# Layer 0 of a two-layer diffusion step: two of four gate chunks computed beside later head groups, modulation pieces spread evenly, rotary products on VectorE

## The chip, the cores and the metric

The kernel runs on one core of one Trainium2 chip. The metric is device time in microseconds (us) from one launch. Engines are named as in the profile: PE is TensorE (PEld its weight load), DVE is VectorE, ACT is ScalarE, POOL is GpSimd, SP issues most transfers.

## The reference, cut to what matters

Tokens are 512 latent ones (four tiles of 128) and 128 context ones (a fifth tile), width 1024. Layer 0 is gated attention, layer 1 a linear recurrence. All of the change lies in layer 0.

```python
sh, sc, g = split(silu(cond) @ ada_w[i] + ada_b[i])        # per layer: 3 x 1024 values for each of two conditions
h = x * (1 + sc) + sh
q, k, v, gate = split(h @ w_in)                            # 1024, 256, 256, 1024 columns
q, k = rms_norm(q), rms_norm(k)                            # per head of 64; 16 query heads, 4 key heads
q, k = rope(q), rope(k)                                    # latent tokens only: x*cos + rotated(x)*sin
o = softmax(q @ k.T / 8) @ v                               # latent: 128 cached + 512 keys; context: 128 keys
x = layer_norm(alpha * x + g * ((o * silu(gate)) @ w_out))
```

## The kernel before, in words

Each float32 weight piece (128x1024, 512 KB) is loaded into a ring of three `raw` buffers and split into a rounded part `whi` (ACT, a cast) and a remainder `wlo` (a subtraction, `split_piece`, L217); each product is three matmuls. Projection weights come in chunks of 256 columns, two pieces each: chunk 0 to 3 are the queries of head groups 0 to 3 (four heads on one key head), chunks 6 to 9 the gate.

The program writes instructions in one order; a scheduler in the compiler may move them a little on each engine, and `keep_in_program_order` pins some. The stages of layer 0 are:

- **Start**: load, modulate, keys and values (`acc`), queries of group 0 (`pmm`, L323 to L325).
- **Lead-in** (`lead_in`): 16 blocks of gate projection (`gps`, L316 to L318, 24 matmuls of 320 columns each; four chunks, each two row halves by two token halves), each followed by a Silu on ACT (L705) into `gs`. Between the blocks the pieces of work in `later` are issued: for the queries of group 0 `rms_prep` (sum of squares on DVE, power -1/2 on POOL, L188, product `qn` on DVE, L518), `rope_apply` (`u` = x*sin on POOL, L531; `r` = x*cos and the sum on DVE, L533 and L535), `q_split`, then transposes (`qps`, `kps`) on PE.
- **Attention** (`att_gen`): for each of four groups one context unit and eight latent units. A unit has fronts (scores `sc`, maximum `nm` on DVE L802, exponential `p` on ACT L805, reciprocal `rc` on DVE, scaling of `p` on POOL L810), backs (transposes `pt` on PE L817, copied to `pts`), and for every second unit the product with the values (`pot`, L736) that is multiplied into `gs` on DVE (`av_out`, L740). Fronts run two units ahead.
- A second stream, `side`, is woven into attention by `weave`: after each step of attention an accumulator grows by `SIDE_B`, and each whole unit lets `side` take one step. It holds, in a row: query projection of group 1 (`q_gen`, `qmm`), four modulation chunks (`ada_gen`, `adaps`, two `raw` pieces each), group 2, four chunks, group 3, four chunks, four chunks, then the first two pieces of the output weights (`wohi`, `wolo`) and the splitting of `gs` into `hhi`, `hlo` (L923, L924).
- **Output projection** (`outp`, L969 to L971), and then layer 1.

PSUM in lead-in and attention: two double banks (`bank2`, scores), one bank for `pot`, three banks (`bank1`) for all else, `pt`, `qmm`, `adaps` and transposes among it.

Of the kernel before, what the change touches and what calls it, by code (L numbers as in the profile page):

```python
# [18 lines left out]
P = 128  # L19
# [14 lines left out]
ADA_CUT = (4, 8, 12)  # L34
# [7 lines left out]
D_LO = 1  # L42
ROOT = False
SIDE_T = 2.2
SIDE_B = 0.7
# [13 lines left out]
class Side:  # L59
# [5 lines left out]
    def step(self):  # L65
        while self.items:
            ready = self.items[0][2:]
            if ready and not ready[0]():
                return False
            try:  # L70
                next(self.items[0][1])
                return True
            except StopIteration:
                self.items.pop(0)
        return False

    def until(self, name):
        while any(i[0] == name for i in self.items):
            assert self.step()

    def finish(self):
        while self.step():
# [50 lines left out]
def hybrid_step(ctx: ExitStack, tc: tile.TileContext, a: dict, o: dict):  # L133
# [158 lines left out]
    def ada_gen(chunks):  # L292
        todo, last = None, None
        for l, c in chunks:
            ps = bank1("adaps")
            ada_mms(ps, l, c, 0)
            if last:
                last()
            last = todo and ada_out(*todo)
            yield  # L300
            ada_mms(ps, l, c, 1)
            yield
            todo = (l, c, ada_row(ps))
        if last:
            last()
        if todo:
            last = ada_out(*todo)
            yield
            if last:
                last()  # L310
                yield

    def feat_mms(ps, w, mt, j, hhi, hlo):
        c, t = slice(mt * P, (mt + 1) * P), slice(*HALVES[j])
        for k in range(KT):
            nc.tensor.matmul(ps[:, :320], w.hi(k)[:, c], hhi[:, k, t], start=(k == 0), stop=False)  # L316
            nc.tensor.matmul(ps[:, :320], w.hi(k)[:, c], hlo[:, k, t], start=False, stop=False)
            nc.tensor.matmul(ps[:, :320], w.lo(k)[:, c], hhi[:, k, t], start=False, stop=(k == KT - 1))  # L318

    def tok_gen(out, w, tt, hhi, hlo):  # L320
        t = slice(tt * P, (tt + 1) * P)
        for k in range(KT):
# [3 lines left out]
            if k % 4 == 3:  # L326
                yield
# [15 lines left out]
    ADA_AT = (0,) + ADA_CUT + (len(ADA),)  # L343
    ADA_B = [ADA[ADA_AT[n]:ADA_AT[n + 1]] for n in range(4)]

# [8 lines left out]
    for c in (0, 6, 7, 8, 9):  # L354
        order.extend(pieces("attn_w_in", c))
    for c in range(3):
        order.extend(pieces("attn_w_in", c + 1))
        order.extend(ada_pieces(ADA_B[c]))
    order.extend(ada_pieces(ADA_B[3]))
# [138 lines left out]
    def rms_prep(ps, n):  # L498
        return rms_apply(ps, n, rms_stat(ps, n, ROOT))

    def rms_stat(ps, n, root=False):
        w = n * CW
        sq = prep.tile([P, 2 * CW], F32, tag="sq", name="sq")
        nc.scalar.activation(sq[:, :w], ps[:, :w], AF.Square)
        ss = tiny.tile([P, 8], F32, tag="ss", name="ss")
        nc.vector.tensor_reduce(ss[:, :4 * n], view(sq, 0, [[HD, 4 * n], [1, HD]]), AX.X, ALU.add)
        rstd = tiny.tile([P, 8], F32, tag="rstd", name="rstd")
        if root:
            nc.scalar.activation(rstd[:, :4 * n], ss[:, :4 * n], AF.Sqrt, bias=eps[:, 0:1], scale=1.0 / HD)
            nc.vector.reciprocal(rstd[:, :4 * n], rstd[:, :4 * n])  # L510
        else:
            rsqrt(rstd[:, :4 * n], ss[:, :4 * n], 1.0 / HD, NORM_EPS)
        return rstd

    def rms_apply(ps, n, rstd):
        w = n * CW
        qn = prep.tile([P, 2 * CW], F32, tag="qn", name="qn")
        nc.vector.tensor_tensor(view(qn, 0, [[HD, 4 * n], [1, HD]]), ps[:, :w].rearrange("p (h d) -> p h d", d=HD),  # L518
                                view(rstd, 0, [[1, 4 * n], [0, HD]]), ALU.mult)
        return qn  # L520

    def rope_apply(qn, tt0, n, cos, sin, g, r=None):
# [8 lines left out]
        nc.gpsimd.tensor_tensor(heads4(u[:, :w], n), heads4(qn[:, :w], n),  # L531
# [55 lines left out]
    def q_gen(c, X):  # L587
        w = Weights("attn_w_in", c)
        yield
        yield  # L590
        pend = None
        for tt0, n in UNITS:
            ps = yield from tok_unit(w, tt0, n, "qmm")
            rstd = rms_stat(ps, n)
            yield
            if pend:
                for i in range(pend[1]):
                    pend[0](i)
                    yield
            qn = rms_apply(ps, n, rstd)  # L600
            r = rope_apply(qn, tt0, n, cosq, sinq, qg)
            yield
            pend = (q_split(r, tt0, n, c % 2, X, bank1), n)
        yield
        for i in range(pend[1]):
            pend[0](i)
            yield
# [11 lines left out]
    def lead_in(att):  # L619
# [40 lines left out]

        def q_job(n):
            tt0, m = UNITS[n]
            r = rope_apply(rms_prep(q0[n], m), tt0, m, cosq, sinq, qg)
# [21 lines left out]
        open_rest()  # L685
        k_rope(2)
        later = [lambda n=n: q_job(n) for n in range(3)] + [lambda: backs.append(split_k(ck, 1, 0))]
        later += [lambda n=n: k_split(n) for n in range(3)]
        step = 0
        for ch in range(6, 10):  # L690
            if ch < 9:
                ws[ch + 1] = Weights("attn_w_in", ch + 1, LEAD_LO)
            w = ws.pop(ch)
            for mt in range(2):
                for j, (t0, t1) in enumerate(HALVES):
                    ps = bank_any("gps")
                    feat_mms(ps, w, mt, j, hhi, hlo)
                    step += 1
                    if step % 2 or not later:
                        settle()  # L700
                    if step % 2 and later:
                        later.pop(0)()
                    if step > 16 - EARLY:
                        next(att)
                    nc.scalar.activation(gs[:, 2 * (ch - 6) + mt, t0:t1], ps[:, :320], AF.Silu)  # L705
# [32 lines left out]
    def av_out(pot, gt):  # L738
        tv = pot[:, :CW]
        nc.vector.tensor_tensor(gt, tv.rearrange("p (a b) -> p a b", a=2) if len(gt.shape) == 3 else tv, gt, ALU.mult)  # L740
# [11 lines left out]
    def prompt_unit(c):  # L752
# [29 lines left out]
        def apply():  # L782
            pot = pop[0].tile([P, 512], F32, tag="po", name="potp")
# [9 lines left out]
    def sample_unit(c, h, qh):  # L793
# [29 lines left out]
        def pair():  # L823
            mine = {k: live.pop(k) for k in list(live)}

            def apply():
                pot = pop[0].tile([P, 512], F32, tag="po", name="pot")
# [8 lines left out]
    def att_gen(side):  # L836
        units = []
        for c in range(4):
            units.append(prompt_unit(c))
            units += [sample_unit(c, 2 * pr + j, qh) for pr in range(2) for qh in range(2) for j in range(2)]  # L840
# [643 lines left out]
```

## Time and profile before

| | |
|---|---|
| time, median of 3 runs | 902.72 us (902.19 to 903.58) |
| the profiled execution, its own time | 903.73 us |
| its span, first to last instruction | 902.0 us |
| PE busy | 851.4 us (94%) |
| DVE, ACT, POOL busy | 533.7, 372.6, 245.9 us |
| mean granted clock of PE | 0.984 |

The span lies inside the execution's time; 1.7 us lie around it. A matmul's end is modelled in the profile, and matmuls overlap, so busy PE time says when it had work, not how fast it went; the pace is read from the distance of starts. The granted clock is a share of full speed: 1.00 is 2.4 GHz, 0.5 the lower level of 1.2 GHz.

### The profile page before, as it was taken

The page shows a single profiled execution, that of the slowest core. Times are in us where ns is not written, and L with a number is a line of the kernel's source. Part 1 is how long each engine was busy: PE and PEld are TensorE (multiplying, and loading weights), DVE is VectorE, ACT ScalarE, POOL GpSimd, SP SyncE. Part 2 cuts the span into 40 slices and gives each one's busy share as a digit, 9 for nine tenths or more (in the row PEclk, how much of TensorE's full clock was granted, in tenths as well). Part 3 has the DMA queues.
Part 4 walks back from the last instruction along what each step waited for, and adds up shares of the span by engine and source line. Part 5 has one row for each costly group of instructions (what it writes and reads, how often), then busy time and mean ns, then how long its engine had stood idle before and what let it go on. Part 6 is the DMA issues. An engine that isn't in the chain of part 4 may idle for free.

```text
span 902.0 us, 19259 instructions
## 1 busy us (share of the span) xinstructions
PE 851.4 (94%) x8116; PEld 745.8 (83%) x8116; DVE 533.7 (59%) x952; ACT 372.6 (41%) x735; POOL 245.9 (27%) x269
## 2 busy tenths in 40 slices
PE   5999899899899899999999999999999999998995
PEld 3679898778768766677889999999999999986774
DVE  3465334654554554577644667585858575859495
ACT  2141445454454655633244444444444444444200
POOL 2016012524434644440000133233232414120110
PEclk9999899999899999999999999999999999998998
DMA  9931220033033046173121322323132323223121
GB/s 319 324 112 37 92 70 25 2 115 121 1 114 121 1 162 212 48 238 135 57 94 48 96 84 78 100 78 94 54 115 65 90 88 88 84 71 136 54 94 70
DMA packets 32678, 89.86 MB, mean 100 GB/s; under 512 B 4400, under 2 KB 11568, under 8 KB 32592
## 3 DMA queue, kind: packets, MB, share of 16 engines
q1 hardware_dynamic: 21984, 71.57, 24.0%
q0 software_dynamic: 3264, 9.51, 3.9%
q10 hardware_dynamic: 7344, 7.55, 2.7%
q8 instruction: 64, 1.05, 0.5%
q14 instruction: 22, 0.18, 0.1%
HBM read 79.44 MB, written 9.18 MB: 98 GB/s over the span
## 4 chain that ended last, share of the span: by engine, by line
PE 76%; DVE 8%; POOL 6%; ACT 4%; DMA 3%; issue 2%; SPq 0%; ACTq 0%; DVEq 0%; POOLq 0%
PE rps L1091 7%; PE rps L1092 6%; PE rps L1093 6%; PE vgps L1081 5%; PE vgps L1082 4%; PE vgps L1083 4%; PE pot L736 3%; PE outp L969 3%; PE outp L970 3%; PE outp L971 3%; PE adaps L259 3%; PE pt L817 2%; PE lv L1221 2%; POOL rstd L188 2%; PE gps L316 2%
## 5 line engine op out<-in xcount | busy, mean ns | idle before, releaser
L1091 PE MATMUL rps<-h1hi,rhi 128*128 128x320 f32 x368 | 117.5, 319 | 0.0
L1092 PE MATMUL rps<-h1lo,rhi 128*128 128x320 f32 x368 | 113.7, 309 | 0.0
L1093 PE MATMUL rps<-h1hi,rlo 128*128 128x320 f32 x368 | 113.5, 308 | 0.0
L810 POOL TENSOR_SCALAR p<-p,rc 128x640 f32<-128x640 f32 x64 | 53.6, 840 | 84.2 <-DVE rc L809 83.0
L805 ACT ACTIVATE p<-sc,nm 128x640 f32<-128x640 f32 x64 | 51.0, 797 | 46.6 <-DVE nm L802 42.4
L1091 PEld LDWEIGHTS rps<-h1hi,rhi 128*128 128x128 f32 x368 | 69.1, 188 | 1.3
L1092 PEld LDWEIGHTS rps<-h1lo,rhi 128*128 128x128 f32 x368 | 69.1, 188 | 0.0
L1093 PEld LDWEIGHTS rps<-h1hi,rlo 128*128 128x128 f32 x368 | 69.1, 188 | 0.0
L1249 POOL COPY At<-near 32x160 f32<-32x160 f32 x32 | 14.0, 438 | 197.5 <-DVE near L1211 196.5
L217 DVE TENSOR_TENSOR rlo<-raw,rhi 128x1024 fp32r<-128x1024 f32 x32 | 46.1, 1441 | 34.0 <-ACT rhi L216 34.0
L802 DVE TENSOR_REDUCE nm<-sc 128x1 f32<-128x640 f32 x64 | 51.9, 818 | 15.7 <-PE sc L710 15.6
L817 PE MATMUL pt<-small,p 128*128 128x128 f32 x320 | 50.3, 280 | 9.7 <-DVE pts L714 6.2
L1199 ACT COPY kc<-A 128x640 f32<-128x640 f32 x40 | 32.2, 805 | 58.8 <-DVE A L1230 50.8
L216 ACT CAST rhi<-raw 128x1024 fp32r<-128x1024 f32 x32 | 33.6, 1048 | 51.9 <-PE rps L1092 46.9
L1081 PE MATMUL vgps<-rhi,h1hi 128*128 128x256 f32 x180 | 51.2, 285 | 1.2 <-ACT h1hi L923 1.2
L817 PEld LDWEIGHTS pt<-small,p 128*128 128x128 f32 x320 | 37.2, 143 | 18.2 <-DVE pts L714 6.8
L1083 PE MATMUL vgps<-rhi,h1lo 128*128 128x256 f32 x180 | 50.4, 280 | 0.4 <-DVE h1lo L924 0.4
L1082 PE MATMUL vgps<-rlo,h1hi 128*128 128x256 f32 x180 | 50.5, 280 | 0.0
L736 PE MATMUL pot<-pts,vv 128*64 128x256 f32 x320 | 46.7, 389 | 0.0
L316 PE MATMUL gps<-hhi,whi 128*128 128x320 f32 x128 | 40.7, 318 | 5.6 <-DVE qn L518 5.6
L709 PE MATMUL sc<-kk,X 128*128 128x320 f32 x128 | 44.1, 353 | 0.4 <-ACT p L805 0.2
L714 ACT COPY pts<-pt 128x512 f32<-128x512 f32 x64 | 35.6, 588 | 16.9 <-PE pt L817 16.9
(259 smaller groups left out, 2450.0 us busy)
## 6 DMA issues: line engine op xcount, KB each, us to landing
raw<-in_ada_w SPq DMA_DIRECT2D x48, 512.0 KB, 4.8
raw<-in_rec_w_in SPq DMA_DIRECT2D x40, 512.0 KB, 3.7
raw<-in_attn_w_in SPq DMA_DIRECT2D x16, 512.0 KB, 4.1
raw<-in_attn_w_out SPq DMA_DIRECT2D x8, 512.0 KB, 4.3
raw<-in_rec_w_out SPq DMA_DIRECT2D x8, 512.0 KB, 3.6
x1d<-y SPq DMA_DIRECT2D x5, 512.0 KB, 3.3
rx<-x1d POOLq DMA_DIRECT2D x20, 128.0 KB, 3.6
x1a<-rx POOLq DMA_DIRECT2D x20, 128.0 KB, 2.7
```

The lines of the kernel that those rows point to most:

```text
L316: nc.tensor.matmul(ps[:, :320], w.hi(k)[:, c], hhi[:, k, t], start=(k == 0), stop=False)
L736: nc.tensor.matmul(pot[j * HD:(j + 1) * HD, :CW], vv[:, slot, c * HD:(c + 1) * HD], moving[j], start=first, stop=last)
L802: nc.vector.tensor_reduce(nm[:, 0:1], sc[:, :, :320], AX.XY, ALU.max, negate=True)
L805: nc.scalar.activation(halves(p[:]), sc[:, :, :320], AF.Exp, bias=nm[:, 0:1], accum_out=su[:, 0:1])
L810: nc.gpsimd.tensor_scalar(p, p, rs[:, 0:1], 1.0, ALU.mult, ALU.mult)
L817: nc.tensor.transpose(pt[:, i * 256 + q * P:i * 256 + (q + 1) * P], ps[q][:, (k0 + i) * P:(k0 + i + 1) * P], ident)
L1081: nc.tensor.matmul(out, h1hi[:, k, t], hi, start=(k == 0), stop=False)
L1082: nc.tensor.matmul(out, h1hi[:, k, t], lo, start=False, stop=False)
L1083: nc.tensor.matmul(out, h1lo[:, k, t], hi, start=False, stop=(k == KT - 1))
L1091: nc.tensor.matmul(ps[:, j, :320], hi[:, k, :], h1hi[:, k, t], start=(k == 0), stop=False)
L1092: nc.tensor.matmul(ps[:, j, :320], hi[:, k, :], h1lo[:, k, t], start=False, stop=False)
L1093: nc.tensor.matmul(ps[:, j, :320], lo[:, k, :], h1hi[:, k, t], start=False, stop=(k == KT - 1))
```

## The change

1. Lead-in computes gate chunks 6 and 7 only (8 blocks). Its other pieces of work are issued one after each block, in another order, and at most one transposition stays open (`LAG`). The sums of squares of all queries of group 0 get one joint power (`q_stats`).
2. Gate chunks 8 and 9 go to `side` (`g_gen`): after its 24 matmuls a block has an exponential on ACT, then on DVE an addition, a reciprocal and a product, in place of the Silu.
3. `side` has one generator, `fill_gen`: segments of group 1, group 2, chunk 8, group 3, chunk 9, each with a given number of modulation pieces (half chunks) set among its steps; the remaining 11 pieces follow the last segment. All weight remainders there are made on DVE; before, POOL made those of the three query chunks.
4. `u`, the product with sin, moves from POOL to DVE in all places.
5. Steps of both streams carry durations, which `weave` compares.
6. In `q_gen` more steps lie between the sum of squares and `qn`. Products into `gs` come two steps later (`D_OUTS`). In each group the context unit stands last, not first.

```diff
-ADA_CUT = (4, 8, 12)
+SEGS = (("q", 1, 4), ("q", 2, 4), ("g", 8, 4), ("q", 3, 3), ("g", 9, 6))
-SIDE_B = 0.7
+SIDE_B = 0.95
+AHEAD_ADA, Q_STEPS = 2, 24
+LAG = 2
...
-def weave(main, side, ratio):
-    acc = 0.0
-    for _ in main:
-        acc += ratio
-        while acc >= 1.0:
-            acc -= 1.0
-            side.step()
+    due, done = 0.0, 0.0
+    for t in main:
+        due += ratio * t
+        while due - done >= 1.0:
+            got = side.step()
+            if got is None:
+                done = due
+                break
+            done += got
...
         u = prep.tile([P, 2 * CW], F32, tag="u", name="u")
-        nc.gpsimd.tensor_tensor(heads4(u[:, :w], n), heads4(qn[:, :w], n),
+        nc.vector.tensor_tensor(heads4(u[:, :w], n), heads4(qn[:, :w], n),
...
+    def g_gen(ch, w):
+        for mt in range(2):
+            for j, (t0, t1) in enumerate(HALVES):
+                ps = bank1("gps")
+                yield from feat_mms(ps, w, mt, j, hhi, hlo)
+                ge = sm.tile([P, 320], F32, tag="ge", name="ge", bufs=1)
+                nc.scalar.activation(ge, ps[:, :320], AF.Exp, scale=-1.0)
+                nc.vector.tensor_scalar(ge, ge, 1.0, 1.0, ALU.add, ALU.mult)
+                nc.vector.reciprocal(ge, ge)
+                nc.vector.tensor_tensor(gs[:, 2 * (ch - 6) + mt, t0:t1], ps[:, :320], ge, ALU.mult)
+            have.add(2 * (ch - 6) + mt)
...
+        def q_stats():
+            ss = rtab.tile([P, NKV * TT], F32, name="ssq")
+            for n, (tt0, m) in enumerate(UNITS):
+                squares(q0[n], m, ss[:, NKV * tt0:NKV * (tt0 + m)])
+            rsqrt(rq, ss, 1.0 / HD, NORM_EPS)
...
-        for ch in range(6, 10):
-            if ch < 9:
-                ws[ch + 1] = Weights("attn_w_in", ch + 1, LEAD_LO)
+        ws[7] = Weights("attn_w_in", 7, LEAD_LO)
+        for ch in (6, 7):
...
+    def fill_gen():
+        for kind, c, n in SEGS:
+            while kind == "q" and front_of[0] < c - 1:
+                yield None
+            w = Weights("attn_w_in", c, (nc.vector, nc.vector))
...
+            for _ in range(AHEAD_ADA):
+                yield next(ada)
+            got = 0
+            for i, t in enumerate(bulk):
+                yield t
+                if got < n - AHEAD_ADA and (i + 1) * (n - AHEAD_ADA + 1) >= (got + 1) * total:
+                    got += 1
+                    yield next(ada)
...
+        yield from ada
```

Where instructions stand now is shown at three places. The first is DVE in the lead-in, from the sums of squares of group 0's queries (`ss`, now `ssq`) on. Before:

```order
68 L506 TENSOR_REDUCE ss<-sq 128x8
69 L533 TENSOR_TENSOR kr<-kr,cosk 128x512
70 L187 TENSOR_SCALAR rs_t<-ss 128x8
71 L535 TENSOR_TENSOR kr<-kr,u 128x512
72 L518 TENSOR_TENSOR qn<-pmm,rstd 128x512
73 L533 TENSOR_TENSOR r<-qn,cosq 128x512
74 L535 TENSOR_TENSOR r<-r,u 128x512
75 L506 TENSOR_REDUCE ss<-sq 128x8
76 L187 TENSOR_SCALAR rs_t<-ss 128x8
```

The same place now:

```order
74 L512 TENSOR_REDUCE ssq<-sq 128x8
75 L222 TENSOR_TENSOR wlo<-raw,whi 128x1024
76 L512 TENSOR_REDUCE ssq<-sq 128x4
77 L192 TENSOR_SCALAR rs_t<-ssq 128x20
78 L222 TENSOR_TENSOR wlo<-raw,whi 128x1024
79 L525 TENSOR_TENSOR qn<-pmm,rq 128x512
80 L538 TENSOR_TENSOR u<-qn,sinq 128x512
81 L540 TENSOR_TENSOR r<-qn,cosq 128x512
82 L542 TENSOR_TENSOR r<-r,u 128x512
83 L576 TENSOR_TENSOR qs_857<-r,qs_857 128x8x64
```

The three sums now come first and share one power (the `rs_t` of 20 columns feeds it), and `u` has joined DVE's row.

The second place is the first query unit inside attention (`ss` is its sum of squares, `qn` the normed queries). DVE before:

```order
121 L506 TENSOR_REDUCE ss<-sq 128x8
122 L802 TENSOR_REDUCE nm<-sc 128x1
123 L187 TENSOR_SCALAR rs_t<-ss 128x8
124 L518 TENSOR_TENSOR qn<-qmm,rstd 128x512
125 L809 RECIPROCAL rc<-su 128x1
126 L533 TENSOR_TENSOR r<-qn,cosq 128x512
```

DVE now, from the same sum on:

```order
131 L512 TENSOR_REDUCE ss<-sq 128x8
132 L192 TENSOR_SCALAR rs_t<-ss 128x8
133 L835 TENSOR_REDUCE nm<-sc 128x1
134 L772 TENSOR_TENSOR gs<-pot,gs 128x256
135 L525 TENSOR_TENSOR qn<-qmm,rstd 128x512
136 L745 COPY pts<-pt 128x256
137 L538 TENSOR_TENSOR u<-qn,sinq 128x512
```

Two other instructions now stand between `rs_t`, which POOL's power waits for, and `qn`, which waits for the power. POOL's row for group 1 before (`p` is the scaling of probabilities):

```order
32 L188 TENSOR_TENSOR rstd<-rs_t,mhalf 128x8
33 L531 TENSOR_TENSOR u<-qn,sinq 128x512
34 L810 TENSOR_SCALAR p<-p,rc 128x640 x3
35 L188 TENSOR_TENSOR rstd<-rs_t,mhalf 128x8
36 L531 TENSOR_TENSOR u<-qn,sinq 128x512
37 L810 TENSOR_SCALAR p<-p,rc 128x640 x3
38 L188 TENSOR_TENSOR rstd<-rs_t,mhalf 128x4
```

POOL's row for the same group now:

```order
21 L843 TENSOR_SCALAR p<-p,rc 128x640 x8
22 L193 TENSOR_TENSOR rstd<-rs_t,mhalf 128x8
23 L843 TENSOR_SCALAR p<-p,rc 128x640 x4
24 L193 TENSOR_TENSOR rstd<-rs_t,mhalf 128x8
25 L843 TENSOR_SCALAR p<-p,rc 128x640 x4
26 L193 TENSOR_TENSOR rstd<-rs_t,mhalf 128x4
```

`u` has left POOL's row; a power is followed by the scalings at once.

The third place is PE at the end of attention, up to the first matmul of the output projection. Before:

```order
1486 L817 MATMUL pt<-small,p 128x128
1487 L736 MATMUL pot<-pts,vv 64x256 x2
1488 L817 MATMUL pt<-small,p 128x128 x6
1489 L736 MATMUL pot<-pts,vv 64x256 x5
1490 L817 MATMUL pt<-small,p 128x128 x12
1491 L736 MATMUL pot<-pts,vv 64x256 x10
1492 L969 MATMUL outp<-wohi,hhi 128x512
```

Now (`pscp`, `ptp` and `potp` are scores, transposes and product of the context unit):

```order
1501 L740 MATMUL pscp<-kk,X_2878 128x128
1502 L741 MATMUL pscp<-klo,X_2878 128x128
1503 L850 MATMUL pt<-small,p 128x128 x12
1504 L767 MATMUL pot<-pts,vv 64x256 x7
1505 L811 MATMUL ptp<-small,pp 128x128 x4
1506 L767 MATMUL pot<-pts,vv 64x256 x3
1507 L767 MATMUL potp<-pts,vv 64x256 x2
1508 L1021 MATMUL outp<-wohi,hhi 128x512
```

The last context unit stands at the very end now, where before latent units stood; the last modulation piece (`adaps`) stands 18 rows ahead of `outp`, before 58.

## Rows read from the trace of the kernel before

**Rows 1.** Busy time by stage, lead-in and attention: PE, PEld, DVE, ACT, POOL; clock.
```profile
77.40:146.90 69.50, 63.88 (x451) 63.71 (x451) 25.43 (x42) 27.20 (x52) 12.68 (x8) 0.95 0.17 54
146.90:382.30 235.40, 222.47 (x1725) 170.95 (x1723) 126.40 (x284) 124.16 (x272) 104.20 (x96) 0.98 0.27 88
```
**Rows 2.** The same view inside the lead-in.
```profile
77.40:88.00 10.60, 10.60 (x74) 10.60 (x74) 5.75 (x11) 3.22 (x6) 6.49 (x5) 1.00 0.01 2
88.00:98.00 10.00, 4.38 (x25) 4.26 (x23) 6.60 (x10) 2.91 (x7) 3.05 (x2) 0.66 0.32 106
98.00:146.90 48.90, 48.90 (x356) 48.85 (x356) 13.08 (x22) 21.07 (x40) 3.13 (x2) 1.00 0.17 55
```
**Rows 3.** The critical chain through the lead-in: start, length, what.
```profile
78.74 2.11 POOL rstd L188
...
87.71 3.41 DVE wlo L217 x2
...
93.85 0.44 DVE qn L518
```
**Rows 4.** PE's waits in attention: us in total, times, longest.
```profile
PE pt L817 <- DVE pts L714: 6.2, 3, 2.4
PE pt L817 <- POOL p L810: 3.3, 4, 2.1
PE qps L576 <- DVE qn L518: 1.2, 1, 1.2
```
**Rows 5.** POOL's timeline at one of these waits.
```profile
225.02 1.65 POOL L188 TENSOR_TENSOR rstd<-rs_t,mhalf 128x8 f32<-128x8 f32 x1 [0.94 <-DVE rs_t L187]
227.47 1.78 POOL L531 TENSOR_TENSOR u<-qn,sinq 128x512 f32<-128x512 f32 x1 [0.80 <-DVE rc L809]
229.23 2.11 POOL L810 TENSOR_SCALAR p<-p,rc 128x640 f32<-128x640 f32 x2
```
**Rows 6.** Busy time and clock round the same wait, columns as in rows 1.
```profile
226.00:236.00 10.00, 7.91 (x54) 7.50 (x54) 4.51 (x9) 3.24 (x7) 5.34 (x5) 0.83 0.00 0
```
**Rows 7.** DVE's groups by line and shape in attention: busy, mean ns, idle before.
```profile
L802 DVE TENSOR_REDUCE nm<-sc 128x1 f32<-128x640 f32 x64 | 51.9, 818 | 15.7 <-PE sc L710 15.6
...
L740 DVE TENSOR_TENSOR gs<-pot,gs 128x256 f32<-128x256 f32 x16 | 6.7, 422 | 16.7 <-PE pot L736 16.7
...
L533 DVE TENSOR_TENSOR r<-qn,cosq 128x512 f32<-128x512 f32 x6 | 6.1, 1014 | 0.0
...
L518 DVE TENSOR_TENSOR qn<-qmm,rstd 128x512 f32<-128x512 f32 x6 | 4.2, 692 | 9.9 <-POOL rstd L188 9.9
```
**Rows 8.** Timelines of DVE and POOL ahead of the lead-in: the keys' norm.
```profile
72.41 1.75 DVE L642 TENSOR_TENSOR kr<-acc,rk 128x256 f32<-128x256 f32 x5 [3.77 <-POOL rk L188]
68.80 3.58 POOL L188 TENSOR_TENSOR rk<-rs_t,mhalf 128x20 f32<-128x20 f32 x1 [0.52 <-DVE rs_t L187]
```
**Rows 9.** DVE's weight remainders from 60 us to the end of the lead-in.
```profile
L217 DVE TENSOR_TENSOR wlo<-raw,whi 128x1024 fp32r<-128x1024 f32 x8 | 10.8, 1356 | 4.4 <-ACT whi L216 4.4
```
**Rows 10.** Reciprocals of one and of 16 columns: shortest, median, longest ns.
```profile
L809 DVE RECIPROCAL rc<-su x64: 142/158/165, 149.9 to 377.1; 128x1 f32<-128x1 f32 x64
L905 DVE RECIPROCAL mx<-mx x1: 253/253/253, 155.7 to 155.7; 128x16 f32<-128x16 f32 x1
```
**Rows 11.** ACT's weight casts and the context unit's exponentials in attention.
```profile
L216 ACT CAST whi<-raw 128x1024 fp32r<-128x1024 f32 x5 | 5.2, 1046 | 2.1 <-DMA raw<-in_attn_w_in 2.1
L765 ACT ACTIVATE pp<-pscp,nmp 128x128 f32<-128x128 f32 x12 | 4.2, 363 | 13.6 <-DVE nmp L761 13.6
```
**Rows 12.** POOL's groups in attention.
```profile
L810 POOL TENSOR_SCALAR p<-p,rc 128x640 f32<-128x640 f32 x64 | 53.6, 840 | 84.2 <-DVE rc L809 83.0 <-PE qmm L324 1.1
...
L531 POOL TENSOR_TENSOR u<-qn,sinq 128x512 f32<-128x512 f32 x6 | 9.7, 1621 | 4.8 <-DVE rc L809 2.4 <-DVE qn L518 2.4
L771 POOL TENSOR_TENSOR pp<-pp,rcp 128x512 f32<-128x512 f32 x4 | 4.2, 1040 | 34.7 <-DVE rcp L770 34.7
```
**Rows 13.** The critical chain in attention: dense runs of transposes and value products.
```profile
182.46 0.87 PE pt L817 x8
...
379.53 2.41 PE pot L736 x20
```

More of the change, by code (lines that the diff above doesn't have):

```diff
@@ L66, in step, with until @@
         while self.items:
-            ready = self.items[0][2:]
+            gen, *ready = self.items[0]
             if ready and not ready[0]():
[L69 to L79, printed above, removed]
+                return None
+            got = next(gen, 0.0)
+            if got != 0.0:
+                return got
+            self.items.pop(0)
+        return None
+    def until(self, test):
+        while not test():
+            assert self.step() is not None
     def finish(self):
-        while self.step():
+        while self.step() is not None:
             pass
 def weave(main, side, ratio):
-    acc = 0.0
-    for _ in main:
-        acc += ratio
-        while acc >= 1.0:
-            acc -= 1.0
-            side.step()
+    due, done = 0.0, 0.0
[7 more added lines that the diff above has]
+            done += got
 class Lane:
@@ L353, in hybrid_step @@
     FIRST = set(order)
-    for c in (0, 6, 7, 8, 9):
+    for c in (0, 6, 7):
         order.extend(pieces("attn_w_in", c))
[L356 to L359, printed above, removed]
+    left_ada = ada_pieces(ADA)
+    for kind, c, n in SEGS:
+        order.extend(pieces("attn_w_in", c))
+        order.extend(left_ada[:n])
+        del left_ada[:n]
+    order.extend(left_ada)
     order.extend(("attn_w_out", nh, i) for nh, i in PIECES)
@@ L782, in apply @@
         def apply():
+            side.until(lambda: have >= {2 * c, 2 * c + 1})
             pot = pop[0].tile([P, 512], F32, tag="po", name="potp")
@@ L826, in apply @@
             def apply():
+                side.until(lambda: 2 * c + h // 2 in have)
                 pot = pop[0].tile([P, 512], F32, tag="po", name="pot")
@@ L838, in att_gen @@
         for c in range(4):
+            units += [sample_unit(c, 2 * pr + j, qh) for pr in range(2) for qh in range(2) for j in range(2)]
             units.append(prompt_unit(c))
-            units += [sample_unit(c, 2 * pr + j, qh) for pr in range(2) for qh in range(2) for j in range(2)]
         AHEAD = 2
@@ L847, in fronts @@
             front_of[0] = c
-            side.until(f"q{c}")
+            side.until(lambda: c in have_x)
             return list(fr)
@@ L1389, in hybrid_step @@
         load_resid(tt)
-    side = Side(("t", tail_gen()))
-    weave(lane.gens[0][0], side, SIDE_T)
+    side = Side([tail_gen()])
+    weave((1.0 for _ in lane.gens[0][0]), side, SIDE_T)
     side.finish()
```

139 lines of the change are left out of this document (74 added, 65 removed).

## The prediction

> **What bounds the kernel now.** I read the stages first. In the stages that the change touches, lead-in and attention, PE has work for 63.88 of 69.50 and 222.47 of 235.40 us [rows 1]; DVE, ACT and POOL are busy for about half of attention or less. So PE sets the time, and what can be won is what PE loses: time in which it waits, and time at the lower clock. The granted clock was 0.95 in the lead-in and 0.98 in attention. A clock share of 0.98 over 235.4 us is 4.7 us of full pace lost, 0.95 over 69.5 is 3.5 us.
>
> Then where. In the lead-in the loss lies in one place: from 88 to 98 us PE runs 25 matmuls at a mean clock of 0.66, while it is dense before and after (356 in 48.9 us, 0.137 us apart) [rows 2]. At that distance 25 take 3.4 us, so 6.6 us are lost. The chain shows why: three times, for one part of the queries after the other, POOL's power (2.11 us the first one) and then DVE's product, with `u` on POOL and two weight remainders (3.41 us) on DVE between them [rows 3]. PE waits for the third product, `qn` at 93.85, since it reads the last PSUM bank that the next gate block needs.
>
> In attention PE's waits name transposes `pt`, 6.2 us behind DVE's copies and 3.3 behind POOL's scaling `p`, and 1.2 before query transposes [rows 4]: 10.7 of the 12.9 us that PE is idle there. What stands ahead of them is a query unit. At one of them POOL makes the power from 225.02 (1.65 us), waits for DVE's product, makes `u` from 227.47 (1.78), and gets to `p` at 229.23: 4.2 us in which no scaling runs [rows 5]. Round it the clock falls to 0.83 [rows 6]; two more of these places look like it. In the same time DVE's in-order row stands still at `qn` (9.9 us for six of them), and `r` beside `u` takes 1.014 us on average, `qn` of the same shape 0.692 [rows 7]; maxima and copies are queued behind both.
>
> **Part 1, lead-in.** Two gate chunks are 192 matmuls of 320 columns. They leave a dense stage and enter another where PE is the bound as well, so the move itself costs and gives nothing; it only spreads cover. What counts is the loss of 6.6 us. Now DVE's row has, from the end of the keys' norm at 74.16 us [rows 8] to the joint power, eight instructions of 512 columns (0.69 each), two of 256 (0.42), one weight remainder (1.36) [rows 7, 9] and one small one (0.16) [rows 10]: 7.9 us, so 82.1. The power of 20 columns took 3.58 us for the keys [rows 8]: 85.7. Four products of 0.69, a cast of some 0.6 (half of 1.05 for 1024 columns [rows 11]) and one subtraction of 0.69 give 89.7. PE has 72 gate matmuls, until 87.8 by the pace of the first stretch (74 in 10.6 us [rows 2]), and a few key transposes. So it waits 1.6 us at most, less where DVE's instructions overlap: 1.0. The second and third parts need no power of their own any more.
>
> At the hand-over to attention there is less cover than before: the first scores come when only one gate block is left, and ACT has a weight cast (1.05 us [rows 11]) between the first exponentials. The trace has no such place; bounds are nothing and two waits like the longest one for `p` (2.1 us [rows 4]). I take 1.5, nearer to one than to none. Sum: -6.6 + 1.0 + 1.5 = **-4.1**, between -6.6 and -1.
>
> **Part 2, query units in attention.** `u` leaves POOL (1.62 us, six times), and with it the wait ahead of it; its weight remainders leave as well [rows 12]. In the place of rows 5 `p` could start at 226.7, 2.5 us earlier, which is more than the longest wait of PE for it (2.1). On DVE a maximum (0.82) and a product of 0.42 [rows 7] now stand between `rs_t` and `qn`, so that 1.2 of the 1.65 us of the power are filled, and `r` no longer collides with `u`. Power and `qn` remain, nine times. I keep 3 of the 10.7 us of waits, and 2 of the 4.7 us of clock: the drops to the lower level stand behind the longest of these waits, and go with them. Sum: -7.7 - 2.7 = **-10.4**; bounds are nothing and -15.4.
>
> **Part 3, new work on DVE in attention.** Six `u` of 0.69 (4.1 us), ten weight remainders of 1.36 (13.6; before, POOL made those), and eight gate blocks with an addition, a reciprocal and a product. No row has a reciprocal of 320 columns. One column takes 0.158 us, 16 take 0.253 [rows 10]: 6.3 ns a column, so 2.2 us for 320 as an estimate; as an ordinary instruction of that size it would be 0.5, between the 0.42 and the 0.69 of rows 7. I take 2.2, since both rows are reciprocals. With 0.5 for each of the two others that is 3.2 us a block, 25.6 in all. DVE then has 126.4 + 43 = 169 us of work in a stage of about 260 (65%). It fits, but a maximum can stand 2.2 us behind a reciprocal. Cover is that fronts run two units ahead: 36 units in 260 us are 7 us each, so 14 us for a chain of scores, maximum, exponential, reciprocal and scaling, of which maximum and scaling take 0.82 and 0.84 [rows 7, 12]. I take **+3** exposed, between nothing and eight times 2.2, 17.6.
>
> One rule speaks against this part. By rows, `r` beside POOL's `u` took 0.32 us longer than alone [rows 7], and two scalings beside DVE's products 2.11 instead of 1.68 [rows 5, 12]: 0.43 more. The Trainium skill (SBUF — State Buffer, section "SBUF: two separate sides") has it that a DVE instruction with two SBUF inputs and a POOL instruction that reads SBUF take one port pair in turn, the later one waiting for the whole of the other; the rows agree in kind. By that page alone each of the 16 moved instructions could hold a scaling for its full length. What it would do here is a rival below.
>
> **Part 4, end of attention.** The last context unit now stands at the very end: maximum 0.69, four exponentials of 0.36, a reciprocal, the scaling `pp` of 1.04 [rows 11, 12], some 3.5 us, and ahead of its exponentials ACT has two casts of output weights, 1.05 each. PE has only 12 transposes (0.109 us each) and 7 products (two records each, 0.12 us a record [rows 13]) as cover: 3.0 us. It waits between 0.5 and 2.6 us; I take **+1.6**. Output weights load later than before, since the last modulation pieces hold the ring longer; the first products need only the first two pieces, and these are cast ahead of the unit. 0 for that, up to +3.
>
> **Sum.** -4.1 - 10.4 + 3 + 1.6 = -9.9. The profiled execution took 903.7 us in all, so 893.8; it stands 1.0 above the median of the runs, so **893 us** as a median. A difference of 0.2%, 1.8 us, is about what a measurement of this kernel can tell from no change.
>
> **Rivals.**
> - *DVE becomes the bound (the other side).* Each of the eight reciprocals holds maxima and copies as `qn`'s wait for the power did, and each shows on PE with its 2.2 us: 17.6 in place of 3, so 893 + 14.6 = **907.6**. For it: a DVE wait of 1.65 us was enough for PE waits of about 2. Against it: in those places POOL was held as well, now it is not. It decides from about 13 us exposed on, six of eight blocks. 0.12 for 903 and more.
> - *DVE and POOL collide anew.* Each of 16 moved instructions costs a scaling 0.43 us and all of it shows: +7, **900**. This is the mechanism of the page named above. Against it: POOL is idle for 84.2 us ahead of its scalings [rows 12], which swallows such a delay mostly. 0.13.
> - *The waits stay.* Moving `u` doesn't help, since the power and `qn` still stand in both rows; only the lead-in gains: 903.7 - 4.1 + 4.6 - 1.0 = **903**, no change. For it: nine powers remain, like the one of 1.65 us in rows 5. Against it: 2.6 of the 4.2 us there are `u` and its wait. 0.13.
> - *More is won.* All waits and clock losses of both stages go and nothing new shows: -6.6 - 15.4, **881**; half way between that and the forecast is likelier, 886. 0.12.
> - The forecast, 888 to 898: 0.50.
>
> **How the numbers follow.** The forecast and the larger gain lie below 900.9, the collision's case mostly, the other two above: faster 0.76, no change 0.12, slower 0.12. The range reaches from 885, inside the larger gain, to 903, which takes in collision and waits that stay; left out are the tip of the one side and DVE as the bound.
>
> **What would show it.** In the profile after: between the start of the gate blocks and the first scores, PE idle for under 3 us and a clock near 1.00 (part 1); PE's waits for `p` and for DVE's copies under 5 us together, and a clock of 0.99 in attention (part 2); reciprocals near 2.2 us, with DVE at some 65% of attention (part 3); PE idle for 1 to 2.5 us ahead of `ptp` (part 4). The prediction is wrong if PE waits longer behind maxima, or if query transposes or score banks take the place of `pt` in the list of waits.

## The result: slower by 0.4%, and the profile after

The changed kernel took 907.38 us (median of 6 runs, 904.83 to 909.01), the kernel before 903.08 beside it (6 runs). The two medians alone lie 0.48% apart; the ratio given for all the runs is 1.0039, with a 95% interval of 1.0024 to 1.0054, and all ratios below are of this kind. Measured once more on another occasion the ratio was 1.0028 (1.0010 to 1.0047). I had forecast 893 and given "slower" 0.12. The profiled execution took 904.83 us, its span 902.7; it is the shortest of the six, and only 1.1 us longer than the profiled execution of the kernel before.

The stages come first again, answering to [rows 1, 2]: lead-in, the ten microseconds that were thin before, attention, one stretch of it, and all behind it. The columns are as there.

```profile
77.40:113.00 35.60, 34.18 (x248) 33.23 (x247) 20.89 (x37) 16.84 (x30) 5.25 (x2) 1.00 0.14 48
88.00:98.00 10.00, 8.58 (x65) 8.26 (x63) 4.47 (x7) 6.12 (x10) 0.00 (x0) 1.00 0.08 24
113.00:381.40 268.40, 254.13 (x1928) 197.29 (x1926) 156.90 (x325) 134.01 (x290) 84.61 (x84) 0.98 0.25 85
305.70:315.90 10.20, 9.59 (x44) 7.64 (x45) 2.73 (x8) 4.19 (x10) 2.64 (x3) 0.50 0.21 73
381.40:902.00 520.60, 499.64 (x5504) 460.07 (x5504) 344.44 (x551) 200.87 (x383) 115.30 (x148) 0.99 0.29 91
```

The lead-in is as forecast: PE idle for 1.42 us in place of 5.62, at a clock of 1.00 in place of 0.95. Attention isn't. PE is idle there for 14.27 us, before for 12.93 [rows 1], and the clock is 0.98 again. Its loss of clock lies in one stretch, 10.2 us at 0.50, the lower level, which cost 5.1. Output projection began at 381.4, only 0.9 earlier than before, and all behind it took 521.3 us in place of 519.7.

Waits and clock don't explain all of this. In lead-in and attention together PE's idle time fell by 2.9 us and the loss of clock by some 3 (5.1 now, 3.5 and 4.7 before by the clocks of [rows 1]), and yet only 0.9 us were won. The rest went into PE's busy time: the same 2176 matmuls kept it busy for 288.3 us in place of 286.4, though they lost less to the clock, so at one clock they took some 5 us more. Ends of matmuls are modelled, so this may be short stops that show as no wait. No run separates it.

PE's waits in attention, to be held against [rows 4] (total, times, longest; the first five of the list, and the three on `pt`):

```profile
PE sc L740 <- ACT p L838: 4.4, 2, 4.1
PE pot L767 <- DVE gs L772: 2.9, 4, 1.1
PE qps L583 <- DVE qs L576: 2.1, 2, 1.4
PE sc L740 <- ACT pp L797: 0.6, 1, 0.6
PE potp L767 <- DVE gs L772: 0.6, 1, 0.6
...
PE pt L850 <- POOL p L843: 0.4, 1, 0.4
...
PE pt L850 <- DVE qn L525: 0.3, 1, 0.3
PE pt L850 <- ACT pts L745: 0.2, 1, 0.2
```

The waits for `pt` fell from 9.5 us to 0.9. In their place stand scores (`sc`) that wait for a bank, value products (`pot`, `potp`) that wait for `gs`, and query transposes. Where the longest comes from is seen in the timeline (start, length, engine, what; idle before it): the hand-over to group 3, and then the tail.

```profile
301.57 0.65 PE L767 MATMUL pot<-pts,vv 128*64 128x256 f32 x2
...
301.93 0.15 DVE L192 TENSOR_SCALAR rs_t<-ss 128x4 f32<-128x4 f32 x1
302.00 1.21 DVE L222 TENSOR_TENSOR wlo<-raw,whi 128x1024 fp32r<-128x1024 f32 x1
302.17 1.92 POOL L193 TENSOR_TENSOR rstd<-rs_t,mhalf 128x4 f32<-128x4 f32 x1 [1.90 <-DVE rs_t L192]
304.12 0.42 DVE L525 TENSOR_TENSOR qn<-qmm,rstd 128x256 f32<-128x256 f32 x1 [0.91 <-POOL rstd L193]
304.46 0.81 DVE L835 TENSOR_REDUCE nm<-sc 128x1 f32<-128x640 f32 x1
...
305.37 0.79 ACT L838 ACTIVATE p<-sc,nm 128x640 f32<-128x640 f32 x1 [3.40 <-DVE nm L835]
...
306.31 0.64 PE L740 MATMUL sc<-kk,X 128*128 128x320 f32 x1 [4.09 <-ACT p L838]
...
375.98 1.94 PE L767 MATMUL pot<-pts,vv 128*64 128x256 f32 x14 [0.96 <-DVE gs L772]
...
380.18 0.65 PE L767 MATMUL potp<-pts,vv 128*64 128x256 f32 x4 [0.61 <-DVE gs L772]
...
381.35 0.50 PE L1021 MATMUL outp<-wohi,hhi 128*128 128x512 f32 x1 [0.52 <-DVE gs L772]
```

Group 3's first two scores were done by 301.6, and both score banks full. Their maxima `nm` stand on DVE behind a remainder and behind `qn` of that group's last query unit, and `qn` waits for POOL's power. So the first maximum starts at 304.46, the exponential follows, and PE gets a bank at 306.31. It is [rows 5] in another place: what was held there was `p`, here it is `nm`. The stretch at half clock begins while PE waits.

DVE's new work (busy, mean ns, idle before), and POOL's scalings:

```profile
L625 DVE RECIPROCAL ge<-ge 128x320 f32<-128x320 f32 x8 | 17.2, 2148 | 0.2
...
L222 DVE TENSOR_TENSOR wlo<-raw,whi 128x1024 fp32r<-128x1024 f32 x9 | 11.7, 1296 | 1.8 <-ACT whi L221 1.8
...
L772 DVE TENSOR_TENSOR gs<-pot,gs 128x256 f32<-128x256 f32 x16 | 6.6, 412 | 7.2 <-PE pot L767 7.2
...
L540 DVE TENSOR_TENSOR r<-qn,cosq 128x512 f32<-128x512 f32 x6 | 4.1, 684 | 0.0
L525 DVE TENSOR_TENSOR qn<-qmm,rstd 128x512 f32<-128x512 f32 x6 | 4.1, 680 | 3.1 <-POOL rstd L193 3.1
...
L843 POOL TENSOR_SCALAR p<-p,rc 128x640 f32<-128x640 f32 x64 | 54.0, 844 | 158.0 <-DVE rc L842 144.3 <-PE pt L850 7.0 <-DVE gcol L285 3.7
```

The reciprocal takes 2.15 us, DVE is busy for 58% of attention, `qn` waits 3.1 us for powers where it waited 9.9 [rows 7], and POOL has much idle time ahead of its scalings. No engine here is short of room.

Single runs scatter more than the difference looked for, and they scatter with PE's clock: in the second measurement the changed kernel's runs at a mean clock of 0.990 took 902.52 and 903.65 us, those at 0.982 took 909.86 to 911.06. The profile above shows a mild case; ratios of medians carry the comparisons below.

### The profile page after: what moved, and what is told of

Its sections match the earlier page's. It is cut to its first block, busy times and chain, and to the rows that moved or that the text cites. A ratio compares the mean times of both kernels' runs of the same rounds, so it can differ in the third digit from the quotient of the medians.

```text
span 902.7 us, 19256 instructions
## 1 busy us (share of the span) xinstructions
PE 853.8 (95%) x8116; PEld 741.6 (82%) x8116; DVE 560.8 (62%) x990; ACT 374.2 (41%) x735; POOL 217.9 (24%) x251
## 4 chain that ended last, share of the span: by engine, by line
PE 81%; DVE 8%; ACT 3%; DMA 3%; POOL 3%; issue 2%; SPq 0%; DVEq 0%; ACTq 0%; POOLq 0%
PE rps L1143 7%; PE rps L1144 6%; PE rps L1145 6%; PE vgps L1133 5%; PE pot L767 5%; PE vgps L1134 4%; PE vgps L1135 4%; PE pt L850 4%; PE adaps L264 3%; PE outp L1021 3%; PE outp L1022 3%; PE outp L1023 3%; PE lv L1273 2%; PE sc L740 2%; PE gps L325 2%
## 5 line engine op out<-in xcount | busy, mean ns | idle before, releaser
L767 PE MATMUL pot<-pts,vv 128*64 128x256 f32 x320 | 50.1, 394 | 3.0 <-DVE gs L772 2.9
L1133 PE MATMUL vgps<-wspare,h1hi 128*128 128x256 f32 x140 | 41.5, 297 | 0.0
```

The costliest lines, as they stand in the source:

```text
L767: nc.tensor.matmul(pot[j * HD:(j + 1) * HD, :CW], vv[:, slot, c * HD:(c + 1) * HD], moving[j], start=first, stop=last)
L1133: nc.tensor.matmul(out, h1hi[:, k, t], hi, start=(k == 0), stop=False)
```

## The experiments

My theory after the two traces: the mechanisms forecast are there, and three losses at fixed places outweigh them, for which my sum had no or too small a term. **Late queries**: group 3's queries are finished in a bunch right ahead of its first scores. **Late products**: with `D_OUTS` 2 the only `pot` bank stays taken until DVE comes to the deferred product, and the splitting of `gs` begins late. **Tail**: the last context unit. The rival is that DVE's new work costs the time. Ratios are to the kernel before, with 95% intervals, and runs of before beside each had a median of 904 to 905 us. The changed kernel stands at 1.0028 to 1.0039; 0.001 is 0.9 us, and differences in us are worked out so.

### One mend at a time

Queries earlier (seven half chunks of modulation moved behind them):

```diff
-SEGS = (("q", 1, 4), ("q", 2, 4), ("g", 8, 4), ("q", 3, 3), ("g", 9, 6))
+SEGS = (("q", 1, 2), ("q", 2, 2), ("g", 8, 2), ("q", 3, 2), ("g", 9, 9))
```

> Seven modulation half chunks leave the segments ahead of group 3's queries and go behind them; nothing else changes. Late queries (PE loses time because group 3's queries are finished in a bunch right ahead of its first scores, whose maxima stand on DVE behind the product qn that waits for POOL's power): the PE wait of 4.1 us for scores at 302 us and the 10.2 us at half clock behind it (5.1 us of pace) are gone, so 9 us less than the changed kernel, about 898, and below the kernel before. DVE's new work (reciprocals, remainders): that work stays, so no change, 906 to 908.

Measured: 902.91 us, 0.9976 (0.9962 to 0.9990), 5 to 6 us less than the changed kernel, where 9 were expected. PE's wait for scores shrank from 4.4 to 0.3 us and output projection began at 376.9. Some of it was given back, since the last pieces now made the output weights late (waits at the start of output projection), and the lower level came back elsewhere: 6.8 us from 164.4 and 6.8 from 376.0 in this profile.

```profile
PE outp L1022 <- POOL wolo L222: 2.4, 2, 1.2
PE outp L1021 <- ACT wohi L221: 1.0, 1, 1.0
```

Products at once:

```diff
-D_OUTS = 2
+D_OUTS = 0
```

> D_OUTS 0: the products into gs follow the value products at once, as in the kernel before. Deferred products (the one pot bank stays taken until DVE gets to the late product, and the splitting of gs starts later): PE's waits of 2.9 us for pot, 0.6 for potp, 0.5 for outp and 1.1 for hlo go, so 4 to 5 us less than the changed kernel, 903. If instead the deferral protects DVE (without it DVE stands in its row waiting for pot, 16.7 us in the kernel before, with maxima behind it): PE waits for maxima and copies come back and the time is the same or longer, 907 to 910.

Measured: 904.20 us, 0.9999 (0.9982 to 1.0016), about 3 us less than the changed kernel. PE's wait of 2.9 us for `pot` is gone from the list. Those for `potp` (0.6) and for `hlo` (1.1) stayed, so they belong to the tail. The wait of 0.5 for `outp` stayed as well, but it belongs to neither: the kernel before has it too.

Context unit of group 3 four units earlier:

```diff
-            units.append(prompt_unit(c))
+            units.insert(len(units) - (4 if c == 3 else 0), prompt_unit(c))
```

> The context unit of group 3 stands four latent units before the end, those of groups 0 to 2 stay last. Tail (the last context unit costs what stands at 374 to 381 us: 1.1 before pot, 0.9 before potp, 0.8 before outp): 2 us less than the changed kernel, 905, and no wait ahead of potp. If the late gs product alone makes the end late: within 0.5 us of the changed kernel, 907.

Measured: 902.67 us, 0.9971 (0.9955 to 0.9987), 5 to 6 us less, more than the 2 expected. In the profile (of a run of 899.24 us, near the shortest of the twelve) output projection begins 3.1 us earlier and `potp` and `hlo` are waited for no longer. What the rest is, this run doesn't show.

The rival, by leaving the eight reciprocals out (the gate is multiplied by 1 + exp(-x) instead):

```diff
-                nc.vector.reciprocal(ge, ge)
```

> Leaves out the eight reciprocals of 320 columns (2.15 us each, 17 us of DVE) from the gate blocks in attention, so that the gate is multiplied by 1 + exp(-x) and not divided by it; the rest stays. DVE's new work as the cause: some 10 us less than the changed kernel, 895 to 898. Late queries or the tail as the cause: the blocks stand elsewhere (230 to 346 us) than the waits that are long, so 0 to 2 us less, 905 to 907.

Measured: 905.66 us, 1.0010 (1.0000 to 1.0021), 1.6 to 2.6 us less than the changed kernel, with the same 4.1 us wait for scores. 17 us of DVE's time are worth some 2 us, so the reciprocals aren't the bound. The remainders that moved to DVE were not left out in any run.

### The three mends together, and each taken back

The changed kernel again, beside the next runs:

> The changed kernel once more, as the reference for the runs beside it and for a second profile. If its loss lies at fixed places (late queries, deferred products, tail): ratio to the kernel before about 1.004 again, and the profile shows the wait of some 4 us for scores near 302 us and waits for pot again. If it was an accident of the stretches at half clock: a ratio under 1.002 and other waits.

It gave 907.18 us, 1.0028, and a wait of 4.1 us for scores and of 2.9 for `pot` again: the losses stand at fixed places.

All three edits, with one constant more:

```diff
-SIDE_B = 0.95
+SIDE_B = 1.05
```

> Earlier queries, products at once, context unit of group 3 in the middle, all together, and SIDE_B 1.05 in place of 0.95, so that the modulation pieces that were moved back don't make the output weights late. If the three losses are separate places, their gains of 5.7, 3.6 and 6.1 us (by the ratios, against the changed kernel's 1.0039) add up in most part: 10 to 15 us less than the changed kernel, 892 to 897. If they are one and the same loss (whichever edit shifts the same collision): no more than the best alone, 901 to 903.

Measured: **893.15 us** (892.25 to 894.21), 0.9871 (0.9853 to 0.9889): 11.7 us under the kernel before, 14 to 15 under the changed one. Lead-in and attention, and what PE still waits for most:

```profile
77.40:113.00 35.60, 34.18 (x241) 33.38 (x240) 21.84 (x37) 14.84 (x27) 5.11 (x2) 0.95 0.15 49
113.00:371.70 258.70, 249.59 (x1950) 197.77 (x1949) 159.45 (x328) 136.16 (x295) 83.71 (x85) 1.00 0.27 88
```

```profile
PE adaps L264 <- DMA raw<-in_ada_w: 1.8, 3, 1.0
PE pt L850 <- DVE pts L745: 1.7, 2, 1.2
PE qps L583 <- DVE qs L576: 1.5, 2, 1.2
```

The clock of attention is 1.00, PE idle for 9.1 us in place of 14.3, with the same work on DVE. Then each mend was taken back by itself. Late queries again (old `SEGS` and `SIDE_B`):

> The kernel with the three mends, but with late queries again (the changed kernel's segments and its SIDE_B 0.95). Late queries as a loss of its own: the wait of some 4 us for scores near 300 us and the half clock behind it are back, 5 to 9 us more than with all mends (893), 898 to 902. If the other two mends also removed this: within 2 us of 893.

901.88 us, 0.9975 (0.9959 to 0.9990): 9.4 us more. The edit takes back the order of the segments and `SIDE_B` at once; what each is worth by itself wasn't run. The wait for scores (5.4 us) is back. The profiled run is the longest of the twelve (906.57 us); in attention it has two stretches of 10.2 us at the lower level, one at the hand-over to group 1, one at group 3, and a third of 3.4:

```profile
168.30:178.50 10.20, 9.92 (x52) 8.13 (x53) 2.43 (x7) 3.33 (x7) 1.60 (x2) 0.50 0.34 104
311.70:321.90 10.20, 9.24 (x43) 7.29 (x44) 3.08 (x9) 4.51 (x10) 2.65 (x3) 0.50 0.29 99
```

Late products again (`D_OUTS` 2):

> The kernel with the three mends, but with products into gs two steps late again (D_OUTS 2). Deferred products as a loss of its own: PE's waits for pot behind gs (about 3 us in all) are back, 3 to 4 us more than 893, 896 to 897. If they mattered only beside the other two: within 1.5 us of 893.

897.60 us, 0.9917 (0.9893 to 0.9941): 4.2 us more. Its profiled run, the longest of the six (901.34 us), shows only 0.9 us of waits for `pot`, and beside them 2.0 for a modulation piece and 6.8 us at the lower level from 364.1, so the size is shown and the path of it only in part.

Context unit last again:

> The kernel with the three mends, but with the context unit of group 3 last again. Tail as its profile prices it (waits before potp, ptp and hlo): 2 to 3 us more than 893, 895 to 896. As the ratio of the run with this edit alone had it: 6 us more, 899.

895.98 us, 0.9899 (0.9882 to 0.9916): 2.5 us more, with the `hlo` wait of 1.1 us and 0.6 for `potp` back. The two intervals overlap, but each of these six runs was longer than each of the mended kernel's four. 9.4, 4.2 and 2.5 make 16.1; changed and mended kernel lie 14 to 15 apart. So the three, `SIDE_B` among the first, account for it within the intervals.

### Is it DVE's row, or the bunch?

Latent units may start before the fifth tile's queries are normed:

```diff
                     pend[0](i)
+                    if tt0 == TS and i:
+                        have_l.add(c)
...
-            side.until(lambda: c in have_x)
+            side.until(lambda: c in (have_l if len(units[u][2]) > 2 else have_x))
```

> The changed kernel, in which the latent units of a group may start as soon as the queries of the four latent tiles are there; only the context unit waits for the fifth tile's. More of the side stream's steps than before are still issued at once ahead of group 3's first scores, but on DVE the first two maxima of group 3 now stand between the sum of squares and the product qn that waits for POOL's power, no longer behind it. DVE's row (the maxima wait behind that product): the wait of 4.1 us for scores falls under 1 us and the half clock behind it goes, 4 to 9 us less than the changed kernel, 898 to 903. The bunch itself (PE simply has no scores in time, whatever the row): the wait stays at 3 us or more, and the time at 906 to 908.

Measured: 901.86 us, 0.9977 (0.9962 to 0.9992), about 5 us less than the changed kernel; PE's wait for scores is 0.3 us in all. On DVE the maximum now follows the sum of squares at once:

```profile
303.29 1.23 DVE L222 TENSOR_TENSOR wlo<-raw,whi 128x1024 fp32r<-128x1024 f32 x1 [2.35 <-ACT whi L221]
304.81 0.42 DVE L512 TENSOR_REDUCE ss<-sq 128x4 f32<-128x256 f32 x1 [0.29 <-ACT sq L511]
305.29 0.82 DVE L837 TENSOR_REDUCE nm<-sc 128x1 f32<-128x640 f32 x1
```

So the long wait was DVE's row, and the gain is about that of the earlier queries in the same kernel (5 to 6 us). The bunch as such costs something too: a wait of 2.3 us for `pt` behind a `qn` and one of 1.1 of the query products for a bank appeared. The half clock didn't go, against the expectation: 6.8 us at 0.50 now stand ahead of the hand-over, from 296.8, behind that wait for `pt`.

### Where the gate's blocks and `u` belong

All gate chunks in the lead-in, first in the changed kernel, then in the mended one (core of the edit):

```diff
-SEGS = (("q", 1, 4), ("q", 2, 4), ("g", 8, 4), ("q", 3, 3), ("g", 9, 6))
+SEGS = (("q", 1, 4), ("q", 2, 4), ("q", 3, 4))
...
-        for ch in (6, 7):
+        for ch in (6, 7, 8, 9):
```

> All four gate chunks stay in the lead-in (16 blocks, Silu on ACT); the rest of the change stays, with modulation pieces only among the queries. Late queries: group 3's queries no longer stand behind a gate chunk, its hand-over wait of 4 us and the 10 us at half clock go, the waits for pot and the tail stay, so 5 to 9 us less than the changed kernel, 898 to 902. DVE's new work (25.6 us less of it in attention): the same time, but then DVE's waits (pt behind copies, qps) shrink too. If attention needs the gate blocks as cover: waits for pt come back and it is 905 to 910.

> The mended kernel with all four gate chunks in the lead-in (products at once, context unit of group 3 in the middle, segments of queries alone with 2, 4 and 4 half chunks of modulation). If the gate blocks beside attention are worth something as cover: 3 us or more over 893. If only the place of the queries matters and DVE has room for the gate's work: within 2 us of 893. If the gate's work on DVE costs by itself: less than 891.

Measured: 902.33 us, 0.9970 (0.9952 to 0.9988), 5 to 6 us less than the changed kernel, without the long wait for scores; and 896.73 us, 0.9905 (0.9884 to 0.9926), 3.1 us more than the mended one (at `SIDE_B` 0.95). This fits gate blocks that cost time in so far as they push the queries back. Where they don't, they may be worth up to 3 us beside attention; the two intervals touch, and `SIDE_B` differs between these two kernels, so this isn't shown.

The kernel before with `u` on DVE, one line:

```diff
-        nc.gpsimd.tensor_tensor(heads4(u[:, :w], n), heads4(qn[:, :w], n),
+        nc.vector.tensor_tensor(heads4(u[:, :w], n), heads4(qn[:, :w], n),
```

> The kernel before with one line changed: u on DVE. My step: 2.6 of the 4.2 us in which POOL runs no scaling go, PE's waits for p and for copies (9.5 us) shrink by two thirds and the half clock with them: 6 to 10 us less than the kernel before, 893 to 897. Waits stay (the power and qn remain in both rows): within 2 us of the kernel before. DVE as the bound: longer by some us.

Measured: 894.77 us, 0.9891 (0.9873 to 0.9909), 9.9 us less. In its profile attention takes 228.3 us in place of 235.4 and the gate stage ends 2.7 earlier. PE's waits for `pt`, against the 9.5 us of [rows 4]:

```profile
PE pt L817 <- DVE pts L714: 3.7, 3, 1.7
PE qps L576 <- DVE qn L518: 2.4, 3, 1.6
PE pt L817 <- POOL p L810: 1.1, 2, 0.8
```

The same line undone in the changed kernel, and in the mended one:

> The changed kernel with one line undone: u on POOL again. If the gain of u on DVE (10 us in the kernel before) is in the changed kernel too and was outweighed by losses elsewhere: 8 to 12 us more than the changed kernel, 914 to 919. If the wider spacing in the query unit had already taken the waits, or if DVE's fuller row eats the gain: within 3 us of the changed kernel, 905 to 910.

> The mended kernel with u on POOL again. If the spacing has taken the waits that u on DVE would take: within 2 us of the mended kernel, 892 to 895. If the changed kernel's three losses only masked u's worth: 6 to 10 us more, 899 to 903.

Measured: 907.60 us, 1.0039 (1.0022 to 1.0056), no difference to the changed kernel; and 897.13 us, 0.9912 (0.9886 to 0.9938), 3.7 us more than the mended one, though these two intervals touch and the six runs reach from 894.13 to 902.51. With `u` on POOL PE's waits for `pt` in the changed kernel's attention are as small as with `u` on DVE:

```profile
PE pt L850 <- POOL p L843: 0.4, 1, 0.4
...
PE pt L850 <- ACT pts L745: 0.2, 1, 0.2
PE pt L850 <- DVE qn L525: 0.2, 1, 0.2
```

So what took the waits for `pt` in the changed kernel wasn't, or wasn't alone, the place of `u`; which other part of the change did it isn't separated. The worth of this line depends on what else waits. Last, the changed kernel's wider spacing alone, in the kernel before, with `u` on POOL:

```diff
                     pend[0](i)
                     yield
+            else:
+                yield
+            yield
             qn = rms_apply(ps, n, rstd)
...
-SIDE_B = 0.7
+SIDE_B = 0.75
```

> The kernel before, u still on POOL, with only the wider spacing of the query units (two more steps of the side stream between the sum of squares and qn; SIDE_B 0.75 in place of 0.7, so that the stream doesn't fall behind). If spacing and u on DVE take one and the same wait (DVE standing at qn behind the power): some 7 to 10 us less than the kernel before, 894 to 897, as u on DVE alone gave. If the gain of u is its own (POOL held by u, scalings behind it): 0 to 3 us less, 901 to 904.

Measured: 902.55 us, 0.9980 (0.9966 to 0.9995), 1.8 us less. Spacing alone doesn't replace `u`. So `u` on DVE is worth 9.9 us in the kernel before. About 2.7 of that lie in the lead-in, where the joint power takes the same loss, and perhaps 1.8 are shared with the spacing. That leaves 5.4 as an estimate by subtraction, beside the 3.7 of the mended kernel. In the changed one nothing of it can be measured.

## Why the prediction was wrong

**Part 1 held in the main.** The lead-in's wait is 1.4 us, PE stands idle for nothing else in it, and the clock is 1.00 in the profile shown. Nine of the thirteen profiles with this lead-in have a stretch of 3.4 us at the lower level there, 1.7 us of pace. At the hand-over to attention PE's longest wait was 0.5 us, less than the 1.5 taken.

**Part 2 is where the sum failed.** The waits that it was about did go: `pt` waits for 0.9 us, within the "under 5 us" of the forecast. That `u` holds them up is shown in the kernel before, where its line alone gave 9.9 us; in the changed kernel they are gone with `u` on POOL too. The step that failed is "I keep 3 of the 10.7 us of waits, and 2 of the 4.7 us of clock: the drops to the lower level stand behind the longest of these waits, and go with them." I took the waits of [rows 4] away and put nothing in their place, though the parts of the change that decide what is late next were in front of me. The segments put chunk 8 and its modulation pieces ahead of group 3's queries; I looked at where PE's work went ("costs and gives nothing; it only spreads cover") and not at when that group's queries are due. That is the largest term that was missing: 5 to 6 us by its mend alone, 9.4 when taken back together with `SIDE_B`. `D_OUTS` had no term at all: about 3 and 4.2 us. The drop of the clock went with the longest wait, as I had it, only to the new one: 10.2 us at 0.50 beside the wait for scores. And "the move itself costs and gives nothing" took it that PE's work stays as long as it was, where PE was busy for some 5 us more at one clock; the cause of that stays open. The sentence on what would make the prediction wrong named it ("if query transposes or score banks take the place of `pt` in the list of waits"), but among the rivals stood only waits that stay, not waits that move.

**Part 3 held.** The reciprocal takes 2.148 us (forecast 2.2 from two rows of one and 16 columns), a gate block on DVE 3.05 us with its addition (0.43) and product (0.48), against 3.2; DVE's load is 58%, not 65%. Exposed are 1.6 to 2.6 us for the reciprocals, where I took +3 for all. One reading was wrong: of the ten remainders POOL had made six, those of the query chunks; the gate's four were made on DVE before as well, in the lead-in [rows 9]. They are new to attention all the same, so no sum changes.

**Part 4 was too small.** PE waited 0.6 us ahead of `potp` and 1.1 for `hlo` behind it, where I had placed one wait ahead of `ptp`; the 0.96 ahead of `pot` belongs to the late products. Putting the unit back at the end cost 2.5 us, against +1.6, and moving it away in the changed kernel gave 5 to 6, most of which is unexplained.

**The rivals.** DVE as the bound gave 907.6, nearly the time measured, by a mechanism that wasn't there: without the reciprocals the time was 905.66. DVE and POOL colliding anew isn't seen in the scalings: 64 of them take 844 ns each, before 840 [rows 12], and `r` takes 684 ns, now that it has no `u` on POOL beside it, where it took 1014 [rows 7]. Single scalings do take up to 1.75 us beside DVE's products, which agrees with the Trainium skill (SBUF — State Buffer, section "SBUF: two separate sides") in kind; POOL's idle time swallows it. But the collision does stand at the place that counts, in the power that `qn` waits for. In the timeline above POOL's power of 128x4 begins at 302.17, while DVE makes the remainder of 302.00 to 303.21, and takes 1.92 us. POOL's three powers of this shape in attention, in the changed kernel, then in the mended one:

```profile
L193 POOL TENSOR_TENSOR rstd<-rs_t,mhalf 128x4 f32<-128x4 f32 x3 | 5.8, 1949 | 2.0 <-DVE rs_t L192 1.9
```

```profile
L193 POOL TENSOR_TENSOR rstd<-rs_t,mhalf 128x4 f32<-128x4 f32 x3 | 3.1, 1017 | 6.3 <-DVE rs_t L192 6.3
```

In three runs (products at once, queries late again, `u` on POOL in the changed kernel) the remainder was done before the power at this hand-over began: it took 1.02 us, and PE's longest wait for scores was 3.5 to 3.6 us. In four (the changed kernel twice, context unit earlier, no reciprocals) the two overlapped: 1.92 us, and a wait of 4.1. By this comparison some 0.5 us of that wait is this rival. Waits that stay: those for `pt` went.

With the three losses mended the kernel takes 893.15 us. That it equals the forecast is partly chance: the mended kernel lacks Part 4's cost and has a faster side stream, which the forecast didn't count, and its PE is still busy for some 4 us more at one clock than in the kernel before.

## What to carry to other kernels

When a change takes a wait away and also moves work between streams, ask for each consumer when its input is now due, and cost that: here the order of the segments, with `SIDE_B`, cost about as much as the line on `u` could win. An instruction that waits for another engine holds everything behind it on its own engine, so look at what stands behind it at the places where a new stage begins, not at the typical unit alone. What an edit is worth depends on what else waits, so a part of a change is worth measuring alone: one line of this one gave 9.9 us in the kernel before, 3.7 in the mended one and nothing in the changed one. And add up waits, clock and busy time against the time itself; what is left over is a term that no list of waits shows.

## What was not expected of the hardware

A wait cost more than its own length: with 4.1 us for scores went 10.2 us at a granted clock of 0.50, 5.1 us of pace, and 6.8 us at 0.50 in three other profiles with the same wait. And the scatter of runs of one kernel went with the granted clock, from 902.52 us at 0.990 to 911.06 at 0.982 in the changed kernel, while the mended one, whose attention ran at 1.00 in its profile, stayed within 892.25 to 894.21 at 0.991 to 0.993. These are four runs only, and with one mend taken back six runs reached from 895.37 to 901.34, so that a kernel with fewer long waits is also steadier isn't shown.
